# Softmax chains and filter taps in a streaming Conformer layer: negated scores, scaling on ScalarE, two banks in block one, a dearer tap behind the maxima

## Chip, cores and metric

One core of one Trainium2 chip. The metric is the device time of one execution in microseconds (us). Engines are TensorE (PE: matmuls; PEld: its weight loads), VectorE (DVE), ScalarE (ACT), GpSimd (POOL) and SyncE (SP, which issues the DMAs). Each engine works through its own instructions strictly in the order in which the program lists them; an instruction that has to wait holds up everything behind it on the same engine.

## What is computed

One layer of a streaming encoder, 2048 prompt tokens and 64 sample tokens, model width 1024, in fp32. The parts that matter here:

```python
u = glu_a * jax.nn.sigmoid(glu_b)                 # 512 channels
y = conv_general_dilated(concat(hist, u), w_dw)   # causal depthwise filter, 31 taps
y = jax.nn.silu(layer_norm(y + b_dw))             # norm over the 512 channels
conv_out = y @ w_out

s = einsum('bqhd,bkhd->bhqk', q, k) * ATTN_SCALE  # 8 heads of 64, ATTN_SCALE = 1/8
s = where(mask, s + rel_bias[...], NEG_INF)       # own chunk of 64 and the 8 chunks before
o = softmax(s) @ v
```

Both branches are gated, added and projected, and a SwiGLU network of inner width 2816 follows.

## The kernel before

**Tiling.** The 2112 tokens go in four blocks, 0 to 575 (sample and 512 prompt tokens) and then 512 each. In the first phase each block passes through the stages q, 0, k, 1, v, 2, 3, g: q, k, v are the attention projections, 0 to 3 are the four groups of 128 GLU channels, each followed by its filter (`convolve`), and g is the two sets of gates. Every fp32 product is three matmuls of high and low parts (`ps<-whi,hh`, `ps<-whi,hl`, `ps<-wlo,hh`), so PE is by far the most loaded engine. The second phase (merge, projections, SwiGLU) starts after the fourth block; the change touches none of its code.

**The filter.** Per block there are 120 taps behind the four first products, of 606 columns in block one (with the sample's and its history) and 512 elsewhere, one DVE instruction each (`y<-u,wd,y`), each reading the sum that the one before wrote. When all 120 of a block are done, `conv_norm` follows: POOL adds the four groups, PE takes the mean (`pm<-s,ones`), DVE subtracts it four times (`y<-y,pm`), ACT squares four times, POOL adds three times (`s<-s,ln`), and PE takes the second mean with a second `pm<-s,ones`.

**Attention.** A head has four query tiles of 128 (in the first block tile widths of 128, 256, 384 and 512 keys, elsewhere 640) and, in block one, a sample tile of 64. Per tile: PE writes the scores `sc`; DVE adds the bias to the score, scales by 0.125 and takes the row maximum, all in one instruction (`pr<-sc,bias`, result in `sm`), then multiplies the maximum by -1 (`sm<-sm`); ACT takes exp with its row sum (`pr<-pr,sm`); DVE inverts the sum and multiplies (`pr<-pr,sm`; in block four ACT does that); PE transposes (`ptp<-ident,pr`), ACT and DVE split that in high and low (`ph`, `pl`), and PE multiplies by the values (`po`). The score tile is one PSUM buffer of two banks, so the scores of a tile wait until the maximum of the tile before has read it. There are 32 such heads and 8 sample heads, 136 maxima in all.

**The order.** Nothing is scheduled at run time. While the program is written, `Stream` keeps a running load of each engine from a table of costs (a 512-wide tap counts 607 ns of DVE). Every 500 ns of PE load, `tick` lets five lanes issue what is due: token norms, projections' follow-up work, attention, the tail (`conv_norm`) and the filter. The filter lane issues up to four taps when the DVE load is less than 2000 ns ahead of PE; attention goes on when DVE is less than 3000 (2500 between score tiles) and ACT less than 4000 ahead. At stage 0 of a block everything left of the block before, taps and `conv_norm`, is forced out; at stage q the same happens with the token tiles not yet normalised (`x_t`). The tile scheduler below may still move instructions by priority.

Of the kernel before, what the change touches and what calls it, by code (L numbers as in the profile page):

```python
# [8 lines left out]
F32 = mybir.dt.float32  # L9
F32R = mybir.dt.float32r  # L10
AF = mybir.ActivationFunctionType
ALU = mybir.AluOpType
# [4 lines left out]
P = 128  # L17
# [26 lines left out]
PE_LAG = 400.0  # L44
TURN_LAG = 2500.0
KN_LAG = 5000.0
X_LAG = 8000.0
ON_ACT = (3,)
ON_POOL = ()
DMA_LAG = 4000.0  # L50
OUT_LAG = 4000.0
# [6 lines left out]
SCORE_ROOM = {"dve": 2500}  # L58
# [530 lines left out]
def streaming_layer(ctx: ExitStack, tc: tile.TileContext, I, O):  # L589
    nc = tc.nc  # L590
    stream = Stream()
    pe, dve, act, gps = (
        Meter(e, n, stream) for e, n in ((nc.tensor, "pe"), (nc.vector, "dve"), (nc.scalar, "act"), (nc.gpsimd, "pool"))
    )
# [44 lines left out]
    wd = const.tile([P, 4, TAPS], F32, name="wd")  # L639
# [90 lines left out]
    ps_a = p1.enter_context(tc.tile_pool(name="ps_a", bufs=1, space=PSUM))  # L730
    wk = p1.enter_context(tc.tile_pool(name="wk", bufs=1))
# [225 lines left out]
    bias = wk.tile([P, 640], F32, name="bias")  # L957
# [203 lines left out]
    def glu(b, ct):  # L1161
# [22 lines left out]
        W.done()  # L1184
        return u

    def convolve(u, y, ct, b):
# [12 lines left out]
        gps.tensor_copy(hist[:, ct], u[:, w - HIST : w])  # L1200
        dve.tensor_scalar(y[:, ct, :n], u[:, :n], wd[:, ct, 0:1], bdw[:, ct : ct + 1], ALU.mult, ALU.add)
        for k in range(1, TAPS):
            dve.scalar_tensor_tensor(y[:, ct, :n], u[:, k : k + n], wd[:, ct, k : k + 1], y[:, ct, :n], ALU.mult, ALU.add)
            yield

    def conv_norm(y, c0, n, t0):
# [91 lines left out]

    def softmax_max(ps, n, w, bias):
        pr = wk.tile([P, 640], F32, tag="pr", name="pr", bufs=8)  # L1300
        sm = wk.tile([P, 4], F32, tag="sm", name="sm", bufs=9)
        nb = ps.shape[1]
        stream.after("dve", "pe")
        dve.tensor_tensor_reduce(
            out=pr[:n, :w].rearrange("p (a b) -> p a b", a=nb), in0=ps, in1=bias.rearrange("p (a b) -> p a b", a=nb),
            scale=0.125, scalar=-3e38, op0=ALU.add, op1=ALU.max, accum_out=sm[:n, 0:1],
        )
        dve.tensor_scalar(sm[:n, 1:2], sm[:n, 0:1], -1.0, None, ALU.mult)
        free = stream.when("dve")
        stream.after("act", "dve")  # L1310
        act.activation(pr[:n, :w], pr[:n, :w], AF.Exp, bias=sm[:n, 1:2], accum_out=sm[:n, 2:3])
        return pr, sm, free, stream.when("act")

    def softmax_scale(pr, sm, n, w, on_act):
# [48 lines left out]
    def spans(b):  # L1363

        if b == "s":
            return 0, SMP, 0, CACHE + SMP
        past = QB if b else 0
        return SMP + QB * b, QB, CACHE + SMP + QB * b - past, QB + past
# [6 lines left out]
            )  # L1375
        return bias

    order, loaded, now = [], {}, {"scored": -1, "finished": -1, "bias": None}
# [21 lines left out]
    def attend(i):  # L1400
        x, h = order[i]
        q0, nq, k0, nk = spans(x)
# [5 lines left out]
        tiles = []  # L1408
        for t in range(0, nq, P):
            n = min(P, nq - t)  # L1410
            ps = ps_a.tile([P, 2, 512], F32, tag="s", name="sc")
            if x not in (0, "s"):
                for j in range(2):
                    for d in range(2):
                        pe.matmul(ps[:, j, :320], q2[:, d, t : t + P], kk[:, t + 320 * j : t + 320 * j + 320], start=d == 0, stop=d == 1)
                w, src, bs = 640, ps[:, :, :320], bias[:, ::-1]
            else:
                w = nk if x == "s" else t + P
                for d in range(2):
                    pe.matmul(ps[:n, 0, :w], q2[:, d, t : t + n], kk[:, :w], start=d == 0, stop=d == 1)  # L1420
                src, bs = ps[:n, 0:1, :w], bias[:n, 64:384][:, ::-1] if x == "s" else bias[:, :w][:, ::-1]
            pr, sm, free, ready = softmax_max(src, n, w, bs)
            tiles.append((pr, sm, n, w))
            if t + P < nq:
                yield free + PE_LAG, SCORE_ROOM
            else:
                fetch(i + 1)
                now["scored"] = i
            if t:
                softmax_scale(*tiles[-2], x in ON_ACT)  # L1430
        yield ready
        softmax_scale(*tiles[-1], x in ON_ACT)
        yield stream.when("act" if x in ON_ACT else "dve") + PE_LAG
        while now["finished"] < i - 1:
            yield lambda: now["finished"] == i - 1
        fetch_v(i + 1)
# [17 lines left out]
        else:  # L1454
# [15 lines left out]
            for jj in seq:  # L1470
# [11 lines left out]
                w = 512 - t0 * P  # L1482
# [39 lines left out]
    for b, stage in ORDER:  # L1522
# [60 lines left out]
    wk = ctx.enter_context(tc.tile_pool(name="wk2", bufs=1))  # L1583
# [136 lines left out]
    for s, (lo, hi) in enumerate(CBLOCKS):  # L1720
        tiles = token_tiles(lo, hi)
# [392 lines left out]
```

## Time and profile before

| | |
|---|---|
| median of 3 runs | 3046.8 us (3046.7 to 3047.27) |
| profiled execution | 3042.59 us, of which the span 3040.8 us |
| mean granted PE clock | 0.986 |
| PE busy | 2934.8 us (97% of the span) |
| PEld, DVE, ACT, POOL busy | 2606.5, 2052.4, 1256.8, 985.3 us |
| HBM traffic | 226 GB/s over the span |

The profile's windows give, for a stretch of time, how long each engine was busy and the clock granted to PE (1.00 is full, 0.50 half). Its waits name the tile that an idle engine waited for and the engine that released it. In the timeline a row has its start, its length, the engine and the instruction; square brackets hold the idle time ahead of it.

### The profile page before, as it was taken

The page shows a single profiled execution, that of the slowest core. Times are in us where ns is not written, and L with a number is a line of the kernel's source. Part 1 is how long each engine was busy: PE and PEld are TensorE (multiplying, and loading weights), DVE is VectorE, ACT ScalarE, POOL GpSimd, SP SyncE. Part 2 cuts the span into 40 slices and gives each one's busy share as a digit, 9 for nine tenths or more (in the row PEclk, how much of TensorE's full clock was granted, in tenths as well). Part 3 has the DMA queues.
Part 4 walks back from the last instruction along what each step waited for, and adds up shares of the span by engine and source line. Part 5 has one row for each costly group of instructions (what it writes and reads, how often), then busy time and mean ns, then how long its engine had stood idle before and what let it go on. Part 6 is the DMA issues. An engine that isn't in the chain of part 4 may idle for free. (4 is left out here: it accounts for less than half of the span.)

```text
span 3040.8 us, 44889 instructions
## 1 busy us (share of the span) xinstructions
PE 2934.8 (97%) x16259; PEld 2606.5 (86%) x16259; DVE 2052.4 (67%) x3835; ACT 1256.8 (41%) x2267; POOL 985.3 (32%) x617
## 2 busy tenths in 40 slices
PE   7989898999999999989999999999999999999998
PEld 4889776888888788878989889999999898999997
DVE  5896678777977895467666755655666756366567
ACT  3324532453254257464444425534444244333332
POOL 1200120101011102355677433247767341333331
PEclk9999998999999999999999999999999999999999
DMA  9888788888997788886444786455556965355554
GB/s 305 268 275 299 230 286 278 275 263 268 305 284 243 247 265 282 253 285 215 149 143 144 231 290 207 157 165 190 182 194 201 342 215 190 118 167 173 166 160 176
DMA packets 487019, 690.98 MB, mean 227 GB/s; under 512 B 38420, under 2 KB 316808, under 8 KB 486797
## 3 DMA queue, kind: packets, MB, share of 16 engines
q1 hardware_dynamic: 474517, 670.72, 67.3%
q10 hardware_dynamic: 12280, 17.39, 1.6%
q8 instruction: 128, 2.10, 0.3%
q14 instruction: 94, 0.77, 0.1%
HBM read 503.79 MB, written 184.19 MB: 226 GB/s over the span
## 5 line engine op out<-in xcount | busy, mean ns | idle before, releaser
L104 POOL TENSOR_TENSOR wlo<-wst,whi 128x1024 fp32r<-128x1024 f32 (+1 forms) x180 | 401.4, 2236 | 491.6 <-ACT whi L104 463.9
L104 PE MATMUL ps<-t,whi 128*128 128x384 f32 (+1 forms) x2112 | 506.1, 324 | 10.0 <-DVE t L104 4.8
L104 PE MATMUL pd<-whi,hid 128*128 128x512 f32 (+1 forms) x1400 | 450.2, 391 | 3.4 <-DVE acc L104 3.4
L104 ACT ACTIVATE whi<-wst 128x1024 fp32r<-128x1024 f32 (+1 forms) x273 | 266.1, 979 | 358.6 <-PE ps L104 123.7
L104 PE MATMUL ps<-b,whi 128*128 128x384 f32 (+1 forms) x1584 | 381.7, 326 | 11.0 <-DVE pw L104 4.0
L104 PEld LDWEIGHTS ps<-t,whi 128*128 128x128 f32 x2112 | 370.7, 189 | 18.4 <-DVE t L104 5.9
L104 DVE SCALAR_TENSOR_TENSOR y<-u,wd,y 128x512 f32<-128x512 f32 (+1 forms) x480 | 369.3, 772 | 6.7
L104 PE MATMUL ps<-hh,whi 128*128 128x512 f32 (+2 forms) x992 | 364.6, 367 | 0.7 <-DVE h L104 0.7
L104 PE MATMUL ps<-hl,whi 128*128 128x512 f32 (+2 forms) x992 | 348.1, 351 | 0.0
L104 PE MATMUL ps<-hh,wlo 128*128 128x512 f32 (+2 forms) x992 | 347.6, 350 | 0.0
L104 DVE TENSOR_TENSOR acc<-acc,pd 128x512 f32<-128x512 f32 (+1 forms) x440 | 290.7, 684 | 80.5 <-PE pd L104 76.9
L104 PE MATMUL ps<-t,wlo 128*128 128x384 f32 (+1 forms) x1056 | 340.8, 323 | 0.0
L104 PEld LDWEIGHTS pd<-whi,hid 128*128 128x128 f32 (+1 forms) x1400 | 258.1, 184 | 64.7 <-DVE acc L104 6.9
L104 PEld LDWEIGHTS ps<-b,whi 128*128 128x128 f32 x1584 | 278.7, 190 | 14.3 <-DVE pw L104 4.3
L104 PE MATMUL pd<-wlo,hid 128*128 128x512 f32 (+1 forms) x700 | 273.7, 391 | 0.0
L104 PE MATMUL ps<-b,wlo 128*128 128x384 f32 (+1 forms) x792 | 257.3, 325 | 0.0
L104 POOL TENSOR_TENSOR r<-t,mhalf 128x8 f32<-128x8 f32 (+3 forms) x68 | 84.4, 1243 | 390.0 <-DVE t L104 380.1
L104 PEld LDWEIGHTS ps<-hh,wlo 128*128 128x128 f32 x992 | 188.6, 190 | 22.7
L104 POOL TENSOR_TENSOR wlo<-wup,whi 128x1024 fp32r<-128x1024 f32 (+1 forms) x64 | 138.2, 2160 | 213.0 <-ACT whi L104 190.7
L104 PEld LDWEIGHTS ps<-hh,whi 128*128 128x128 f32 x992 | 189.3, 191 | 19.7 <-issue 1.9
L104 PEld LDWEIGHTS ps<-hl,whi 128*128 128x128 f32 x992 | 189.3, 191 | 15.5 <-issue 1.4
L104 PEld LDWEIGHTS ps<-t,wlo 128*128 128x128 f32 x1056 | 199.3, 189 | 0.6
(217 smaller groups left out, 5717.5 us busy)
## 6 DMA issues: line engine op xcount, KB each, us to landing
whi<-w_din_h SPq DMA_DIRECT2D x72, 512.0 KB, 5.8
wlo<-w_din_l SPq DMA_DIRECT2D x72, 512.0 KB, 7.0
wst<-sum_d SPq DMA_DIRECT2D x131, 256.0 KB, 2.9
wmod<-in_w_ada SPq DMA_DIRECT2D x48, 512.0 KB, 6.7
sum_d<-ws SPq DMA_DIRECT2D x88, 256.0 KB, 3.2
wst<-in_w_ffn_in SPq DMA_DIRECT2D x85, 256.0 KB, 3.4
wst<-in_w_in SPq DMA_DIRECT2D x40, 512.0 KB, 7.1
wst<-in_w_ffn_in SPq DMA_DIRECT2D x37, 512.0 KB, 5.3
```

The lines of the kernel that those rows point to most:

```text
L104: return f(*args, **kw)
```

## The change

1. The score instruction takes scale -0.125 and a minimum: the minimum of the negated scores is minus the maximum, so it is directly the bias of exp, which now runs with scale -1. 136 DVE instructions `sm<-sm` go.
2. The scaling by the inverted sum runs on ACT in all blocks: 104 `pr<-pr,sm` leave DVE and are added to ACT (64 of 128x640, the others in block one).
3. In block one a score buffer holds two tiles, one in each bank, and the second is emitted without waiting for the maximum of the first.
4. Each tap adds 110 ns to the emission's DVE load on top of its 607.
5. The first tap emitted after a maximum is told to stand behind that maximum on DVE; the taps after it follow, since they form a chain.

PE has the same 16027 instructions in another order, SP the same 1908. DVE goes from 3837 to 3599, ACT from 2176 to 2280, POOL from 622 to 620 (two `wlo` move to DVE).

```diff
-ON_ACT = (3,)
+    def behind(one):
+        return tc.issue_after(one.ins) if one is not None else nullcontext()
...
         for k in range(1, TAPS):
-            dve.scalar_tensor_tensor(y[:, ct, :n], u[:, k : k + n], wd[:, ct, k : k + 1], y[:, ct, :n], ALU.mult, ALU.add)
+            with behind(now.pop("least", None)):
+                dve.scalar_tensor_tensor(y[:, ct, :n], u[:, k : k + n], wd[:, ct, k : k + 1], y[:, ct, :n], ALU.mult, ALU.add)
+            stream.load["dve"] += 110.0
...
-        dve.tensor_tensor_reduce(
+        now["least"] = dve.tensor_tensor_reduce(
...
-            scale=0.125, scalar=-3e38, op0=ALU.add, op1=ALU.max, accum_out=sm[:n, 0:1],
+            scale=-0.125, scalar=3e38, op0=ALU.add, op1=ALU.min, accum_out=sm[:n, 0:1],
         )
-        dve.tensor_scalar(sm[:n, 1:2], sm[:n, 0:1], -1.0, None, ALU.mult)
...
-        act.activation(pr[:n, :w], pr[:n, :w], AF.Exp, bias=sm[:n, 1:2], accum_out=sm[:n, 2:3])
+        act.activation(pr[:n, :w], pr[:n, :w], AF.Exp, bias=sm[:n, 0:1], scale=-1.0, accum_out=sm[:n, 1:2])
...
-        dve.reciprocal(sm[:n, 3:4], sm[:n, 2:3])
-        if on_act:
-            stream.after("act", "dve")
-            act.activation(pr[:n, :w], pr[:n, :w], AF.Copy, scale=sm[:n, 3:4])
-        else:
-            dve.tensor_scalar(pr[:n, :w], pr[:n, :w], sm[:n, 3:4], None, ALU.mult)
+        stream.after("dve", "act")
+        dve.reciprocal(sm[:n, 2:3], sm[:n, 1:2])
+        stream.after("act", "dve")
+        act.activation(pr[:n, :w], pr[:n, :w], AF.Copy, scale=sm[:n, 2:3])
...
-            ps = ps_a.tile([P, 2, 512], F32, tag="s", name="sc")
+            if x != 0 or t % (2 * P) == 0:
+                both = ps_a.tile([P, 2, 512], F32, tag="s", name="sc")
+            ps = both if x != 0 or t % (2 * P) == 0 else both[:, 1:]
...
-            if t + P < nq:
+            if x == 0 and t % (2 * P) == 0:
+                yield stream.load["pe"], SCORE_ROOM
+            elif t + P < nq:
                 yield free + PE_LAG, SCORE_ROOM
```

How this moves instructions is seen at three places. The first is DVE at the first head of block two. `ISA pr,sm<-sc,bias` is the maximum (after the change, the minimum) of a score tile, `ISA sm` the reading of its accumulator, and `y<-u,wd,y` a tap. Before:

```order
L104 TENSOR_TENSOR A_173<-A_173,cols 128x2x2x2
L104 SCALAR_TENSOR_TENSOR y<-u,wd,y 128x512 x12
L104 ISA pr,sm<-sc,bias 128x640
L104 ISA sm 128x1
L104 SCALAR_TENSOR_TENSOR y<-u,wd,y 128x512
L104 TENSOR_SCALAR sm<-sm 128x1
L104 SCALAR_TENSOR_TENSOR y<-u,wd,y 128x512
L104 ISA pr,sm<-sc,bias 128x640
```

And now, at the same head:

```order
L103 SCALAR_TENSOR_TENSOR u<-tb,ps 128x512
L103 TENSOR_SCALAR y<-u,wd,cols 128x512
L103 COPY R<-pa 128x256
L103 TENSOR_TENSOR A_173<-pa,cols 128x2x2x2
L103 TENSOR_TENSOR A_173<-A_173,cols 128x2x2x2
L103 ISA pr,sm<-sc,bias 128x640
L103 ISA sm 128x1
L103 RECIPROCAL sm<-sm 128x1
L103 ISA pr,sm<-sc,bias 128x640
L103 ISA sm 128x1
L103 ISA pr,sm<-sc,bias 128x640
```

The run of twelve taps that stood directly ahead of the head's first maximum stands behind its maxima now.

The second place is PE at the end of stage q of block two, where the two means of block one's `conv_norm` stand (`pm<-s,ones`; `ps` are projections, `sc` scores of a head of block one). Before, the second mean stood here, 70 rows behind the first:

```order
L104 MATMUL ps<-whi,hh 128x512
L104 MATMUL ps<-wlo,hh 128x512
L104 MATMUL ps<-whi,hl 128x512
L104 MATMUL pm<-s,ones 128x512
L104 MATMUL sc<-kk,q_3947 128x256 x2
```

Now both stand here:

```order
L103 MATMUL ps<-whi,hl 128x512
L103 MATMUL pm<-s,ones 128x512
L103 MATMUL sc<-kk,q_4037 128x128 x2
L103 MATMUL sc<-kk,q_4037 128x256 x2
L103 MATMUL pm<-s,ones 128x512
L103 MATMUL ps<-hh,whi 128x512
```

Only two score tiles stand between the two means.

The third place is PE at the first head of block four. Before, six products stood between one score tile and the next:

```order
L104 MATMUL ps<-hh,wlo 128x512
L104 MATMUL sc<-kk,q_10960 128x320 x4
L104 MATMUL ps<-hh,whi 128x512
L104 MATMUL ps<-hl,whi 128x512
L104 MATMUL ps<-hh,wlo 128x512
L104 MATMUL ps<-hh,whi 128x512
L104 MATMUL ps<-hl,whi 128x512
L104 MATMUL ps<-hh,wlo 128x512
L104 MATMUL sc<-kk,q_10960 128x320 x4
```

Now all four score tiles (16 matmuls) stand together, with the first transposes behind them:

```order
L103 MATMUL ps<-hh,wlo 128x512
L103 MATMUL sc<-kk,q_10838 128x320 x16
L103 MATMUL ptp<-ident,pr 128x128 x2
L103 MATMUL pt<-ident,u 30x128
L103 MATMUL ptp<-ident,pr 128x128 x6
L103 MATMUL ps<-hh,whi 128x512
```

The products that lay between the score tiles stand ahead of them and behind the transposes.

More of the change, by code (lines that the diff above doesn't have):

```diff
@@ L1185, in glu @@
         return u
+    now = {"scored": -1, "finished": -1, "bias": None}
+    def behind(one):
+        return tc.issue_after(one.ins) if one is not None else nullcontext()
     def convolve(u, y, ct, b):
@@ L1300, in softmax_max, with softmax_scale @@
         pr = wk.tile([P, 640], F32, tag="pr", name="pr", bufs=8)
-        sm = wk.tile([P, 4], F32, tag="sm", name="sm", bufs=9)
+        sm = wk.tile([P, 3], F32, tag="sm", name="sm", bufs=9)
         nb = ps.shape[1]
         stream.after("dve", "pe")
-        dve.tensor_tensor_reduce(
+        now["least"] = dve.tensor_tensor_reduce(
             out=pr[:n, :w].rearrange("p (a b) -> p a b", a=nb), in0=ps, in1=bias.rearrange("p (a b) -> p a b", a=nb),
-            scale=0.125, scalar=-3e38, op0=ALU.add, op1=ALU.max, accum_out=sm[:n, 0:1],
+            scale=-0.125, scalar=3e38, op0=ALU.add, op1=ALU.min, accum_out=sm[:n, 0:1],
         )
-        dve.tensor_scalar(sm[:n, 1:2], sm[:n, 0:1], -1.0, None, ALU.mult)
         free = stream.when("dve")
         stream.after("act", "dve")
-        act.activation(pr[:n, :w], pr[:n, :w], AF.Exp, bias=sm[:n, 1:2], accum_out=sm[:n, 2:3])
+        act.activation(pr[:n, :w], pr[:n, :w], AF.Exp, bias=sm[:n, 0:1], scale=-1.0, accum_out=sm[:n, 1:2])
         return pr, sm, free, stream.when("act")
-    def softmax_scale(pr, sm, n, w, on_act):
-        dve.reciprocal(sm[:n, 3:4], sm[:n, 2:3])
-        if on_act:
-            stream.after("act", "dve")
-            act.activation(pr[:n, :w], pr[:n, :w], AF.Copy, scale=sm[:n, 3:4])
-        else:
-            dve.tensor_scalar(pr[:n, :w], pr[:n, :w], sm[:n, 3:4], None, ALU.mult)
+    def softmax_scale(pr, sm, n, w):
+        stream.after("dve", "act")
+        dve.reciprocal(sm[:n, 2:3], sm[:n, 1:2])
+        stream.after("act", "dve")
+        act.activation(pr[:n, :w], pr[:n, :w], AF.Copy, scale=sm[:n, 2:3])
     def load_qk(h, q0, nq, k0, nk):
@@ L1376, in load_bias @@
         return bias
-    order, loaded, now = [], {}, {"scored": -1, "finished": -1, "bias": None}
+    order, loaded = [], {}
     def attention(b):
@@ L1429, in attend @@
             if t:
-                softmax_scale(*tiles[-2], x in ON_ACT)
+                softmax_scale(*tiles[-2])
         yield ready
-        softmax_scale(*tiles[-1], x in ON_ACT)
-        yield stream.when("act" if x in ON_ACT else "dve") + PE_LAG
+        softmax_scale(*tiles[-1])
+        yield stream.when("act") + PE_LAG
         while now["finished"] < i - 1:
```

## The prediction

> **What bounds the kernel now.** I read the page first, then the windows, then the waits of PE, and then the timeline at each long wait.
>
> ```profile
> span 3040.8 us, 44889 instructions
> PE 2934.8 (97%) x16259; PEld 2606.5 (86%) x16259; DVE 2052.4 (67%) x3835; ACT 1256.8 (41%) x2267; POOL 985.3 (32%) x617
> PE 40%; DVE 1%; DMA 1%; issue 0%; ACT 0%; POOL 0%; SPq 0%; DVEq 0%; POOLq 0%; ACTq 0%
> ```
>
> PE is busy for 2934.8 of 3040.8 us and holds nearly all of the chain that ended last. The change leaves PE its 16027 instructions. So the time can only change where PE stands idle (106 us in all) or runs at half clock; DVE and ACT work counts only where PE waits for it.
>
> ```profile
> 190.00:300.00 110.00, 102.71 (x717) 97.51 (x718) 85.23 (x194) 45.39 (x106) 3.32 (x8) 0.94 0.85 284
> 300.00:400.00 100.00, 88.88 (x525) 74.80 (x524) 70.55 (x184) 51.95 (x116) 22.70 (x23) 0.93 0.79 261
> 400.00:500.00 100.00, 92.40 (x466) 72.86 (x466) 75.22 (x166) 27.24 (x65) 10.23 (x9) 0.93 0.92 291
> 500.00:600.00 100.00, 91.01 (x479) 75.19 (x478) 82.95 (x169) 36.26 (x66) 8.07 (x8) 0.95 0.77 253
> 600.00:700.00 100.00, 98.95 (x577) 85.59 (x576) 71.46 (x177) 52.42 (x109) 14.42 (x12) 1.00 0.87 272
> 800.00:900.00 100.00, 99.19 (x527) 82.05 (x526) 85.57 (x165) 41.72 (x75) 13.96 (x12) 1.00 0.90 273
> ```
>
> The columns are window, length, busy PE, PEld, DVE, ACT, POOL, clock, DMA share and GB/s. From 190 to 600 PE misses 7.29 + 11.12 + 7.60 + 8.99 = 35 us and the clock is 0.93 to 0.95. From 600 on it misses one per cent at full clock. The attention of the first blocks is where something can be had; the attention of blocks three and four can only lose.
>
> ```profile
> PE sc L104 <- DVE sm L104: 19.8, 8, 8.0
> PE ptp L104 <- DVE pr L104: 5.0, 4, 3.3
> PE ps L104 <- ACT hh L104: 4.8, 1, 4.8
> PE pt L104 <- DVE x_t L104: 3.5, 1, 3.5
> ```
>
> These are PE's waits from 190 to 620 (total, times, longest). 24.8 us are softmax chains, the rest of the list is the token norm of the next block. I call the five places A (187.8), E (352.4), B (422.7), C (477.3) and D (505), and ask for each stretch:
>
> ```profile
> 187.82:201.00 13.18, 4.99 (x15) 3.08 (x15) 12.74 (x32) 3.74 (x10) 0.00 (x0) 0.62 1.02 376
> 352.40:363.00 10.60, 2.26 (x10) 1.85 (x10) 5.45 (x15) 5.01 (x13) 3.94 (x4) 0.61 1.07 300
> 422.70:430.00 7.30, 3.43 (x11) 2.43 (x11) 5.57 (x17) 2.58 (x7) 0.70 (x1) 0.76 0.27 78
> 477.30:485.00 7.70, 4.37 (x16) 3.12 (x15) 6.24 (x15) 1.63 (x5) 1.13 (x2) 0.75 1.01 405
> 505.00:516.00 11.00, 2.09 (x6) 1.69 (x7) 10.61 (x21) 0.96 (x3) 0.00 (x0) 0.66 0.29 105
> ```
>
> A stretch costs its idle time, and what its matmuls lose to the half clock: nothing of the busy time at least, half of it at most. A: 8.2 to 10.7, E: 8.3 to 9.5, B: 3.9 to 5.6, C: 3.3 to 5.5, D: 8.9 to 10.0. Together 32.6 to 41.3 us, middle 37.
>
> At D the cause is plain, and at A it is of the same kind:
>
> ```profile
> 187.89 5.26 DVE L104 SCALAR_TENSOR_TENSOR y<-u,wd,y 128x606 f32<-128x606 f32 x6
> 193.06 0.28 DVE L104 CUSTOM_DVE_ANT_0 pr<-sc,bias 128x128 f32<-128x128 f32 x1
> 193.41 0.79 PE L104 MATMUL sc<-kk,q 128*128 128x256 f32 x2 [5.59 <-DVE sm L104]
> ```
> ```profile
> 502.77 9.41 DVE L104 SCALAR_TENSOR_TENSOR y<-u,wd,y 128x512 f32<-128x512 f32 x12
> 512.10 0.82 DVE L104 CUSTOM_DVE_ANT_0 pr<-sc,bias 128x640 f32<-128x640 f32 x1
> 512.98 1.43 PE L104 MATMUL sc<-kk,q 128*128 128x320 f32 x4 [8.00 <-DVE sm L104]
> ```
>
> Six taps (5.26 us), and twelve (9.41 us), stood on DVE ahead of the maximum for which the second score tile waits. At C the taps stand between the steps of a sample tile's chain:
>
> ```profile
> 477.51 0.48 DVE L104 CUSTOM_DVE_ANT_0 pr<-sc,bias 64x320 f32<-64x320 f32 x1
> 480.17 0.37 DVE L104 TENSOR_SCALAR pr<-pr,sm 64x320 f32<-64x320 f32 x1
> 480.69 0.36 PE L104 MATMUL ptp<-ident,pr 64*128 64x64 f32 x3 [3.33 <-DVE pr L104]
> ```
>
> **The change, part by part.** The prices:
>
> ```profile
> L104 DVE SCALAR_TENSOR_TENSOR y<-u,wd,y 128x512 f32<-128x512 f32 x360 | 268.4, 748 | 4.8
> L104 DVE CUSTOM_DVE_ANT_0 pr<-sc,bias 128x640 f32<-128x640 f32 x96 | 78.6, 819 | 26.2 <-PE sc L104 23.2 <-DMA bias<-rb_d 1.1 <-PE ptp L104 1.0
> L104 DVE TENSOR_SCALAR pr<-pr,sm 128x640 f32<-128x640 f32 x64 | 38.1, 595 | 0.8
> L104 DVE TENSOR_SCALAR sm<-sm 128x1 f32<-128x1 f32 x128 | 18.9, 148 | 1.0
> L104 ACT ACTIVATE pr<-pr,sm 128x640 f32<-128x640 f32 x128 | 104.6, 827 | 104.2 <-DVE sm L104 102.9 <-ACT gate L104 0.8
> L104 ACT ACTIVATION_READ_ACCUMULATOR pr<-pr,sm 128x1 f32 x128 | 23.9, 187 | 0.0
> L104 DVE TENSOR_SCALAR h<-pt,A,B 128x128 f32<-128x128 f32 x107 | 37.4, 401 | 4.1 <-PE pt L104 4.1
> L104 DVE TENSOR_TENSOR y<-y,pm 128x512 f32<-128x512 f32 x16 | 9.9, 681 | 1.3 <-PE pm L104 1.3
> L104 ACT ACTIVATE hh<-h 128x512 fp32r<-128x512 f32 x24 | 14.8, 626 | 12.2 <-DVE h L104 10.6 <-PE ps L104 1.5
> L104 POOL TENSOR_TENSOR s<-s,ln 128x512 f32<-128x512 f32 x12 | 15.6, 1297 | 83.7 <-ACT ln L104 83.4
> L104 POOL TENSOR_TENSOR r<-t,mhalf 128x8 f32<-128x8 f32 x32 | 61.0, 1906 | 146.9 <-DVE t L104 145.5 <-DVE sm L104 1.4
> ```
>
> PE's pace, for work in its order, is that of two products in a row, 0.23 us from start to start:
>
> ```profile
> 502.20 0.39 PE L104 MATMUL ps<-hh,whi 128*128 128x512 f32 x1
> 502.43 0.39 PE L104 MATMUL ps<-hl,whi 128*128 128x512 f32 x1
> ```
>
> *Negated scores and scaling on ACT.* DVE loses 18.9 us of `sm<-sm`, 38.1 of `pr<-pr,sm` at 128x640, and the smaller shapes; ACT gains 64 x 0.83 = 53 us at 128x640. ACT is busy for 41% of the span, DVE for 67%, PE's work lies over both, so by themselves these are worth nothing outside the waits. Inside a chain the negation saves 0.15 us per tile, while the scaling costs 0.827 on ACT where it cost 0.595 on DVE: 0.23 more, but no longer behind taps. Taken as zero per tile; bounds -0.15 and +0.23 over 104 tiles if every chain were exposed, so -16 and +24, and hardly any is. Freeing DVE should shorten the small waits between the five places. Idle time there is 35 - 32.6, some 3 us on the lower counting, and I take 2 of it.
>
> *Taps behind maxima, and the 110.* They take the taps away from B, C and D. At B the first two scores of the head now stand earlier, 24 us of PE work ahead of the next two: saved 4.7 (middle). At C eleven taps instead of nineteen stand between two maxima, and some 20 matmuls of 0.23 us stand between scores and transposes where one stood: saved 4.4. At D no tap stands ahead of or between the four maxima. Late next are the maxima themselves: each further score tile waits for 0.82 + 0.08 us, and a reciprocal that waits for exp (0.83 + 0.19) stands ahead of the second. So 3 us stay: 9.4 - 3 = 6.4 saved. At A, with its two banks, a filter's first product and two `wlo` stand ahead of the first minimum instead of six taps, but now all four scores and ten transposes stand together with nothing in between, so that the whole chain of four tiles is exposed. I leave 7.4 of 9.4: saved 2, bounds 0 and 5.
>
> *What is forced out later.* A dearer tap means that fewer are emitted per step: the taps of block one end ten maxima later, and its `conv_norm` falls to the end of stage q of block two, where it is forced. The two `pm` stand two score tiles apart (six short matmuls). Between them must run on DVE the first two of the four `y<-y,pm` (2 x 0.68), ACT's square of the second (0.6, as `hh` of the same size), then three `s<-s,ln` on POOL (3 x 1.30), with an `r<-t,mhalf` of 1.91 between the second and third: 1.4 + 0.6 + 3.9 + 1.9 = 7.8 us, less 0.4 of PE work, plus 1 by half clock: **8.4 lost**. Least would be 5 (if `r` is done early), most 11.
>
> E is replaced: the third tile of tokens (`x_t`) still has its DMA six SP issues behind a head's q and k loads, instead of ten, and its eight transposes stand directly before products that need them; I leave 7 of 8.9, saved 2. The fourth tile's eight transposes now stand directly before its products in blocks two, three and four, where there were products between them: eight `h` at 0.40 us on DVE, the first four of which and a split (0.6) PE must await: 2.2 us, three times: **6.6 lost**, bounds 2 and 10.
>
> *First heads and the last.* At block four's first head the four score tiles stand together, where six products lay between them. Three waits of 0.9 us, and 2 us at the transposes: 4.7 lost. The last head's 20 transposes stand 1.4 us of work behind its scores, where 6.1 us stood: 3 lost. Both are bounded by 2 and 10 together with the clock.
>
> The sum: saved 4.7 + 4.4 + 6.4 + 2 + 2 + 2 = 21.5; lost 8.4 + 6.6 + 4.7 + 3 = 22.7. The profiled execution of 3042.6 would become **3043.8**, and with the 4.2 us by which the median lies above the profiled one, 3048.
>
> [...] At B a longest wait of 3.21 us goes with a clock of 0.76 over 7.3 us (the stretches above). [...]
>
> **The rivals.**
>
> *F, faster: the late work overlaps.* The waits of stage q follow each other within some 20 us. While PE stands at `pm`, DVE and ACT finish the fourth tile's norm, so that its 2.2 goes; and with A's chain at its better bound (3 more), E gone (7 more) and first heads free of waits (4), the sum is 16 better: some 3032. For it: DVE is 57 us less busy. Against it: an engine in strict order waits itself, for PE's `pm`.
>
> *S, slower: ACT becomes the bound of exposed heads.* Four tiles of exp, accumulator and scaling take 4 x (0.83 + 0.19 + 0.83) = 7.4 us of ACT behind the first maximum, where the DVE scaling ran beside exp. Where only some 4 us of PE work stands between the last score and the last transposes (first heads of blocks two, three and four, the head before stage q's end, the last) this adds 3 us each, with the clock 4: five times, 15 to 20, so some 3065. It decides from the point at which those heads have less PE work than ACT needs. For it: all scores at A, D and the first head of block four are contiguous. Against it: ACT stands idle for 104.2 us ahead of these instructions.
>
> *N: the order doesn't help.* If B, C and D wait for something else that the releaser hides (the projection's `u`, a bias DMA), 15.5 saved are gone: 3063.
>
> **How the numbers follow.** My forecast (3048, own range 3038 to 3058) has 0.42, F 0.30, S 0.20, N 0.08. The range takes F's better part and S's: 3018 to 3076. A measurement of this kernel can tell about 0.2% (6 us) from no change. Faster by more than that: F, and a quarter of the forecast's chance: 0.40. Within: half of the forecast's chance and a little of F: 0.23. Slower: the rest, 0.37.
>
> **What the new profile would show.** D: the wait of 8.00 gone, two or three of 0.9 to 1.5 in its place. C and B: no wait over 1 us. Near the end of stage q of block two: a wait of `pm` for POOL's `s` of 6 to 9 us, the longest of the run. Block four's first head: three waits `sc<-sm` of 0.9. If ACT `pr` is named ahead of many `ptp`, S holds. The prediction is wrong if `pm` isn't waited for, or if PE loses more than 10 us from 600 to 1225 beside what it lost.

## The result

| kernel | median, us | ratio to before, 95% interval |
|---|---|---|
| before | 3046.8 (15 runs) | |
| changed | 3053.7 (15 runs) | 1.0024 (1.0017 to 1.0031) |

The change costs 7 us. The profiled execution of the changed kernel took 3055.7 us, 13.1 more than that of before; half of that difference is not the change's doing, as the table of losses below shows. Its page:

```profile
span 3053.9 us, 44730 instructions
PE 2942.5 (96%) x16259; PEld 2613.0 (86%) x16259; DVE 2001.3 (66%) x3597; ACT 1323.4 (43%) x2371; POOL 975.0 (32%) x615
PE 40%; DVE 1%; DMA 1%; issue 0%; ACT 0%; POOL 0%; SPq 0%; DVEq 0%; POOLq 0%
```

DVE is busy for 51 us less and ACT for 67 more, as the instruction counts had it, and PE still holds the chain. The windows answer those of before:

```profile
190.00:300.00 110.00, 104.32 (x739) 98.92 (x740) 86.24 (x170) 57.07 (x130) 2.53 (x5) 0.97 0.85 280
300.00:400.00 100.00, 82.81 (x449) 70.57 (x449) 66.24 (x162) 53.74 (x123) 22.59 (x27) 0.88 0.75 247
400.00:500.00 100.00, 97.26 (x534) 76.35 (x533) 78.93 (x154) 34.88 (x75) 11.33 (x11) 1.00 0.90 295
500.00:600.00 100.00, 97.27 (x513) 79.33 (x513) 75.24 (x141) 49.72 (x87) 7.22 (x8) 1.00 0.93 294
```

From 400 to 600 PE gained 11 us of busy time, at full clock; from 300 to 400 it lost 6 and clock. The end of the first phase, half of block four, is where the rest went. The first line below is of before, the second of the changed kernel:

```profile
1040.00:1226.00 186.00, 183.99 (x961) 154.92 (x959) 140.04 (x290) 109.91 (x190) 22.38 (x16) 1.00 0.85 270
```
```profile
1040.00:1237.00 197.00, 184.34 (x932) 153.77 (x930) 134.66 (x251) 108.51 (x188) 22.73 (x16) 0.97 0.80 249
```

The same stretch of the program takes 197 us with 12.7 of idle time, where it took 186 with 2.0.

For all kernels of this study I add up the idle time of PE and half of the time for which it was busy at half clock, between the same products of the main loop, from each trace. "Start" ends at some 185 us, ahead of the first head; "four" is split at 1040 us of before. The last column is the total; the spans less this total agree within 2 us of 2911 for before, changed and the fastest kernel of the study, so this is where the difference lies. The half is an estimate: in the trace of before two products of 512 columns in a row start 0.43 us apart at half clock (363.32 and 363.75) and 0.23 at full clock (502.20 and 502.43).

| lost by PE, us | start | block one | stage q of block two | rest of two | three | four, to 1040 | four, rest | second phase | total |
|---|---|---|---|---|---|---|---|---|---|
| before | 22.3 | 15.2 | 13.6 | 26.5 | 1.8 | 5.5 | 2.3 | 41.8 | 129 |
| changed | 28.8 | 12.8 | 21.1 | 6.1 | 6.7 | 4.2 | 18.6 | 43.8 | 142 |

Each row is one execution, and the start tells how far one execution can be trusted. Its losses all lie in PE's first 564 matmuls, which are the same in every kernel of this study, and yet these losses go from 19.9 to 29.4 us over the 14 traces: 19.7 to 22.1 of idle time, and 0 to 7.9 by half clock. So the 6.5 us between the two starts above are no part of the change.

The waits of PE over the whole of the changed kernel (those of its start and of the second phase left out):

```profile
PE sc L103 <- DVE sm L103: 10.9, 12, 3.8
PE sc L103 <- DMA kk<-k_d: 8.9, 6, 2.2
PE ps L103 <- ACT hh L103: 8.3, 5, 2.4
PE pt L103 <- DVE x_t L103: 8.1, 6, 2.2
...
PE pm L103 <- POOL s L103: 5.9, 3, 3.2
...
PE ptp L103 <- ACT pr L103: 4.5, 8, 1.0
```

The scores' waits for a maximum fell from 19.8 to 10.9 us and the longest from 8.0 to 3.8. The waits for the loads of the keys (`kk`) grew from 2.3 to 8.9 us, and the norm's mean (`pm`) is new on the list. The transposes' wait for the scaled tile, 5.6 us behind DVE's `pr` before, is 4.5 behind ACT's.

### The profile page after: what moved, and what is told of

Same layout as the page of the kernel before. It is cut to its first block, busy times and chain, and to the rows that moved or that the text cites. A ratio compares the mean times of both kernels' runs of the same rounds, so it can differ in the third digit from the quotient of the medians.

```text
span 3053.9 us, 44730 instructions
## 1 busy us (share of the span) xinstructions
PE 2942.5 (96%) x16259; PEld 2613.0 (86%) x16259; DVE 2001.3 (66%) x3597; ACT 1323.4 (43%) x2371; POOL 975.0 (32%) x615
## 5 line engine op out<-in xcount | busy, mean ns | idle before, releaser
L103 PE MATMUL ps<-b,whi 128*128 128x384 f32 (+1 forms) x1584 | 382.1, 327 | 10.9 <-DVE pw L103 4.0
L103 ACT ACTIVATE pr<-pr,sm 128x640 f32<-128x640 f32 (+3 forms) x272 | 200.8, 747 | 145.7 <-DVE sm L103 142.9
L103 PEld LDWEIGHTS ps<-hh,whi 128*128 128x128 f32 x992 | 189.9, 191 | 19.7 <-issue 2.4
```

What stands on the lines that cost most here:

```text
L103: return f(*args, **kw)
```

## The experiments

Every kernel was timed beside the kernel before on the same chip, with medians of before from 3045.7 to 3046.8. The medians of two kernels are compared in the text; the ratios, which weigh all runs of a kernel against those of before on the same chip, put some of these differences lower, and where that matters it is said. Theory E says that the emission decides: taps behind the maxima gain, a dearer tap packs other work together and loses. Theory S says that ScalarE's scaling is the loss. A table of all losses by stage stands behind the twelfth run.

**The extra cost not in block four.**

```diff
-            stream.load["dve"] += 110.0
+            stream.load["dve"] += 110.0 if b < 3 else 0.0
```

> The changed kernel, with the extra 110 ns of a tap left out in block four alone; its order up to block four's first filter is that of the changed kernel. In the profile of the changed kernel PE loses 12.7 us idle and some 6 us by half clock from 1040 us to the end of the first phase, where the kernel before lost 2.3 and 0. Theory E (the dearer tap packs block four's heads together: four score tiles in a row, q and k loads late): most of these 16 us come back, so 10 to 16 us below the changed kernel, some 3040, 4 to 8 below the kernel before. Theory S (the scaling and its place on ScalarE make exposed heads longer): block four scaled on ScalarE before already, so nothing of it differs; 0 to 3 us come back.

3039.3 us, ratio 0.9977 (0.9968 to 0.9986): 14.4 below the changed kernel, as theory E had it. Windows of the same stretch, and the only wait of PE that is listed for it:

```profile
1034.00:1219.00 185.00, 182.35 (x959) 154.67 (x957) 140.16 (x259) 110.55 (x191) 22.62 (x16) 1.00 0.86 271
```
```profile
PE sc L103 <- DVE sm L103: 0.3, 1, 0.3
```

Idle time falls from 12.7 to 2.7 us, the clock is whole again, and the loads of the keys no longer come late. Ahead of that stretch, block four loses 5 us more than in the changed kernel (9.2 for 4.2). Up to block four's first filter the two kernels are the same program, and their losses from block one to block three differ by up to 2.6 us: less than that in a single stage says nothing.

**The extra cost nowhere.**

```diff
-            stream.load["dve"] += 110.0
```

> The changed kernel without the extra 110 ns in any block: taps are emitted as early as before, still behind the maxima. Theory E: block four as in the run above (10 to 16 us back), and the two means of block one's norm stand 19 us of work apart again, so the wait of pm for s near 386 us (3.2) and that of sc ahead of it (3.8) with their half clock (some 4) go: another 5 to 10, but the filters' taps come back ahead of some maxima (6 ahead of one at block three, 4 at block four's first head): 2 to 5 lost. In sum 12 to 20 below the changed kernel: some 3037, 10 below the kernel before. Theory S: within 4 us of the changed kernel.

3035.4 us, 0.9959 (0.9946 to 0.9973): 18.3 below the changed kernel, inside theory E's range. Stage q of block two loses 6.6 us instead of 21.1. The rest of block two loses 15.4 instead of 6.1, and block one itself 18.9 instead of 12.8: there the dearer tap is worth something.

**The rule left out.**

```diff
-            with behind(now.pop("least", None)):
+            if True:
```

> The changed kernel without the rule that a tap stands behind the maximum emitted ahead of it; the 110 stays. In the order 12 taps stand directly ahead of block two's first maximum again, 7 ahead of the very first and 7 ahead of block four's first. Theory E: D comes back at its length before (8.0 us of wait and 2 of half clock, less the 2.0 that stay now): 7 to 8 lost, A 2 to 4 lost, block four's first head 3 to 5 more: 12 to 17 us above the changed kernel, some 3067. Rival: the taps' place doesn't matter, since DVE has 57 us less to do and gets through them in time: within 3 us of the changed kernel.

3063.0 us, 1.0055 (1.0043 to 1.0068): 9.3 above the changed kernel. At block two's first head:

```profile
503.03 9.41 DVE L103 SCALAR_TENSOR_TENSOR y<-u,wd,y 128x512 f32<-128x512 f32 x12
...
512.36 0.82 DVE L103 CUSTOM_DVE_ANT_0 pr<-sc,bias 128x640 f32<-128x640 f32 x1
...
513.24 1.44 PE L103 MATMUL sc<-kk,q 128*128 128x320 f32 x4 [8.00 <-DVE sm L103]
```

D is back to the hundredth (8.00 us), though DVE has its 51 us less to do. So a shorter queue does not help a maximum that stands behind twelve taps. I expected block four to lose 3 to 5 as well; it lost 11.3 instead of 18.6, which is why the sum stayed below 12.

**The scaling back on VectorE in blocks one to three.**

```diff
-        stream.after("act", "dve")
-        act.activation(pr[:n, :w], pr[:n, :w], AF.Copy, scale=sm[:n, 2:3])
+        if on_act:
+            stream.after("act", "dve")
+            act.activation(pr[:n, :w], pr[:n, :w], AF.Copy, scale=sm[:n, 2:3])
+        else:
+            dve.tensor_scalar(pr[:n, :w], pr[:n, :w], sm[:n, 2:3], None, ALU.mult)
...
-        softmax_scale(*tiles[-1])
-        yield stream.when("act") + PE_LAG
+        softmax_scale(*tiles[-1], x == 3)
+        yield stream.when("act" if x == 3 else "dve") + PE_LAG
```

> The changed kernel with the scaling of blocks one to three back on VectorE (595 ns for 128x640 there, against 827 on ScalarE). The taps' cost, the negated scores, the two banks and the rule stay. Theory E: the places move (the two means of block one's norm stay 1.9 us of work apart), the sum hardly: within 5 us of the changed kernel, block four's first head 3 to 6 better as its four score tiles don't stand in one row. Theory S: the chains shorten by 0.23 us a tile and ScalarE's queue by 57 us: 8 to 15 us below the changed kernel.

3036.5 us, 0.9964 (0.9952 to 0.9976): 17.2 below the changed kernel, beyond either. But 12.8 of it stand in the rest of block four (5.8 lost instead of 18.6), whose own scaling didn't change: its heads are no longer packed, presumably since the emission reaches them with other loads. This run can't tell the two theories apart; the eighth can.

**The rule alone, in the kernel before.**

```diff
+            with behind(now.pop("least", None)):
...
-        dve.tensor_tensor_reduce(
+        now["least"] = dve.tensor_tensor_reduce(
```

> The kernel before with one part of the change alone: the first tap emitted after a maximum stands behind that maximum. No taps stand directly ahead of the very first maximum (6 before) nor of block two's first (12 before); the two means of block one's norm stay 15.4 us of work apart, block four's first head stays spread. Theory E (the rule is what gains, the dearer tap what loses): A, C and D give back 10 to 17 us: 3030 to 3037. Rival (the gain needs a VectorE that has less to do): 0 to 4 us below the kernel before, since its 57 us more of work now stand elsewhere in the same chains.

3036.3 us, 0.9972 (0.9961 to 0.9983): 9.4 below before on the same chip (3045.7), at the lower edge of what theory E had. The rest of block two falls from 26.5 to 13.8. One part of the change is a gain by itself.

**One tile per score buffer.**

```diff
-            if x != 0 or t % (2 * P) == 0:
-                both = ps_a.tile([P, 2, 512], F32, tag="s", name="sc")
-            ps = both if x != 0 or t % (2 * P) == 0 else both[:, 1:]
+            if True:
+                both = ps_a.tile([P, 2, 512], F32, tag="s", name="sc")
+            ps = both
...
-            if x == 0 and t % (2 * P) == 0:
-                yield stream.load["pe"], SCORE_ROOM
-            elif t + P < nq:
+            if t + P < nq:
```

> The changed kernel with one query tile per score buffer in block one, as before. The means of block one's norm stand 6.5 us of work apart instead of 1.2. Theory E: A's four scores wait for each other's maxima, 2 to 4 us lost there; the wait of sc (3.8) and pm (3.2) near 386 us shrinks by 3 to 6; block four stays as it is in the changed kernel. In sum within 4 us of the changed kernel, 3050 to 3057. Rival (two banks are worth a chain's length at each of block one's eight heads): 6 to 12 us above it.

3046.0 us, 0.9995 (0.9986 to 1.0004): 7.7 below the changed kernel, neither of the two. In the changed kernel the two banks lose: with one, block one loses 15.1 us instead of 12.8, but stage q of block two 17.3 instead of 21.1 and the rest of two 2.6 instead of 6.1.

**The extra cost in blocks two and three alone.**

```diff
-            stream.load["dve"] += 110.0
+            stream.load["dve"] += 110.0 if b in (1, 2) else 0.0
```

> The changed kernel with the extra 110 ns of a tap in blocks two and three alone. Theory E: the means of block one's norm stand 19.2 us of work apart again, so PE loses at stage q of block two what it lost in the run without any extra (6.6 us) and not what it lost in the one without it in block four (20.5), but some 4 more ahead of it, as there: 8 to 11 below that one, some 3030, and 5 or so below the run without any extra, since the three filters behind keep their order. Rival (where the taps of block one go is of no account, its stalls come back elsewhere): as the run without it in block four, 3037 to 3041.

3031.7 us, 0.9960 (0.9947 to 0.9972): 7.6 below the run without it in block four, a little under theory E's 8 to 11, and level with the run without any (3.7 by the medians, nothing by the ratios, 0.9960 and 0.9959). Stage q of block two loses 5.5 us and block one 20.4, as in the run without any (6.6 and 18.9), where the run without it in block four has 20.5 and 10.5. So in block one the dearer tap gains some 9 us, and pays some 15 for them at stage q.

**The same with the scaling of blocks one to three on VectorE.** The edits of the fourth and the seventh run together.

> The run before in this list, with the scaling of blocks one to three on VectorE. Theory E: the place of the scaling is worth little by itself: within 4 us of the run with the scaling on ScalarE. Theory S: 8 to 15 us below it, near 3018, as four tiles of exp and scaling would be 7.4 us of ScalarE behind the first maximum of each head.

3017.8 us, 0.9916 (0.9901 to 0.9930): 13.9 below the seventh run and 28 below before, the fastest kernel of the study. Theory S is right in size here, theory E wrong. But the mechanism is not the one I gave it: in the seventh run PE waits for ScalarE's scaling (`ptp` behind ACT's `pr`) for 1.8 us in all, from 190 to 1220.

```profile
PE ps L103 <- ACT hh L103: 7.4, 4, 2.4
PE pm L103 <- POOL s L103: 6.2, 2, 5.5
PE sc L103 <- DMA kk<-k_d: 6.0, 7, 2.1
...
PE ptp L103 <- ACT pr L103: 1.8, 5, 0.6
```

What it waits for is other work. In the eighth run (190 to 1200) the key loads are gone from the list, and the waits for the mean fall to 2.7, while those for a maximum grow from 3.2 to 8.3 and those for `x_t` from 1.5 to 4.0:

```profile
PE sc L103 <- DVE sm L103: 8.3, 9, 2.8
PE ps L103 <- ACT hh L103: 5.0, 6, 2.2
PE pt L103 <- DVE x_t L103: 4.0, 1, 4.0
PE pm L103 <- POOL s L103: 2.7, 2, 2.3
```

One of these waits can be followed, the split `hh` of block three's tokens. In the seventh run:

```profile
665.77 2.31 DVE L103 TENSOR_SCALAR h<-pt,A,B 128x128 f32<-128x128 f32 x7
665.89 1.55 ACT L103 ACTIVATE pr<-pr,sm 128x640 f32<-128x640 f32 x2
667.34 0.61 ACT L103 ACTIVATE hh<-h 128x512 fp32r<-128x512 f32 x1
...
668.00 0.50 PE L103 MATMUL ps<-whi,hh 128*128 128x512 f32 x1 [1.98 <-ACT hh L103]
```

Two scalings stand on ScalarE ahead of `hh`, but they hardly delay it: of the seven `h` on DVE, some 0.32 us apart, `hh` reads the first four, the last of which ends at 667.12, 0.2 us before `hh` starts. In the eighth run `hh` (658.15) has projection work (`kn`) and no scaling directly ahead of it, and PE waits half as long:

```profile
657.68 0.59 ACT L103 ACTIVATE kn<-ps 128x512 f32<-128x512 f32 x1
...
658.15 0.63 ACT L103 ACTIVATE hh<-h 128x512 fp32r<-128x512 f32 x1
...
658.84 0.49 PE L103 MATMUL ps<-whi,hh 128*128 128x512 f32 x1 [0.97 <-ACT hh L103]
```

So what differs is the order of the work around the wait, and why VectorE is the better place for the scaling stays open. That it is holds in three pairs of runs: 17.2 us between the changed kernel and the fourth run, 13.9 here, and 6.0 without any extra cost (the second run and the tenth below).

**The rule and the negated scores, in the kernel before.** The rule's edit as in the fifth run, and:

```diff
-            scale=0.125, scalar=-3e38, op0=ALU.add, op1=ALU.max, accum_out=sm[:n, 0:1],
+            scale=-0.125, scalar=3e38, op0=ALU.add, op1=ALU.min, accum_out=sm[:n, 0:1],
...
-        dve.tensor_scalar(sm[:n, 1:2], sm[:n, 0:1], -1.0, None, ALU.mult)
...
-        act.activation(pr[:n, :w], pr[:n, :w], AF.Exp, bias=sm[:n, 1:2], accum_out=sm[:n, 2:3])
+        act.activation(pr[:n, :w], pr[:n, :w], AF.Exp, bias=sm[:n, 0:1], scale=-1.0, accum_out=sm[:n, 2:3])
```

> The kernel before with two parts: taps behind the maxima, and negated scores (136 short VectorE instructions less). The scaling is as before, one tile per score buffer, no extra cost of a tap. The order stands close to that of the rule alone (3036.3). Theory E (an instruction taken off VectorE is worth only what its chain's exposure is): 0 to 4 us below the rule alone, 3032 to 3037. Rival (each of 136 negations at 0.15 us lies on PE's path): 15 to 20 us below it.

3047.7 us, 0.9999 (0.9991 to 1.0008): 11.4 above the rule alone (8 by the ratios), where both expectations had it below. Taking 136 instructions off VectorE cost time. The rest of block two loses 23.2 instead of 13.8: 3.1 us more of idle time and 6.3 more by half clock. The longest wait there is in a sample tile's chain:

```profile
472.19 0.74 DVE L104 SCALAR_TENSOR_TENSOR y<-u,wd,y 128x512 f32<-128x512 f32 x1
...
473.06 0.73 DVE L104 SCALAR_TENSOR_TENSOR y<-u,wd,y 128x512 f32<-128x512 f32 x1
473.71 0.37 DVE L104 TENSOR_SCALAR pr<-pr,sm 64x320 f32<-64x320 f32 x1
...
474.23 0.55 PE L104 MATMUL ptp<-ident,pr 64*128 64x64 f32 x3 [3.44 <-DVE pr L104]
```

This is C of the kernel before, with taps between the steps again and a wait of 3.44. The rule only moves taps behind a maximum, not behind the steps that follow it. But the rule alone has such a wait as well, of 3.23 us at 443.90, so this chain doesn't make the difference; the losses come from several smaller waits and the clock behind them, and which change of the order causes them was not found.

**The fastest without any extra cost.**

```diff
-            stream.load["dve"] += 110.0 if b in (1, 2) else 0.0
```

> The fastest kernel so far (3017.8: scaling on VectorE in blocks one to three, two banks, negated scores, the rule, the extra 110 ns in blocks two and three) without the 110 in any block. If the 110 is worth something there because it keeps taps from between the heads of blocks two and three: 3 to 8 us above it, 3021 to 3026. If it was only ever a loss: 0 to 5 below it.

3029.4 us, 0.9944 (0.9928 to 0.9959): 11.6 above it (8.5 by the ratios). The dearer tap gains in blocks two and three, more than expected: block three loses 8.4 us without it and 1.6 with it, block four's first half 6.6 against 1.9.

**The fastest with one bank.** The edit of the sixth run.

> The fastest kernel so far with one query tile per score buffer in block one. The two means of block one's norm stand 15.5 us of work apart, as before the change, so nothing is packed there. If two banks gain where no stall hides it: A's chain and block one's other heads lose 3 to 8 us, 3021 to 3026. If they gain nothing, as in the run with one bank in the changed kernel (7 us below the changed kernel): 3012 to 3018.

3034.7 us, 0.9959 (0.9947 to 0.9971): 16.9 above it (13 by the ratios), more than twice what was expected. The same two banks that lost 7.7 us in the changed kernel gain 16.9 here. But block one itself loses less with one bank (9.6 for 12.5): the difference stands at stage q of block two (19.0 for 11.0) and in block three (10.3 for 1.6), whose heads have one tile per buffer in both kernels. So what the two banks gain here, too, comes by the order.

**The fastest with block one's scaling on ScalarE.**

```diff
-softmax_scale(*tiles[-2], x == 3)
+softmax_scale(*tiles[-2], x in (0, "s", 3))
...
-yield stream.when("act" if x == 3 else "dve") + PE_LAG
+yield stream.when("act" if x in (0, "s", 3) else "dve") + PE_LAG
```

> The fastest kernel so far with the scaling of block one (and, as ever, block four) on ScalarE, that of blocks two and three on VectorE. It tells where the 14 us between ScalarE and VectorE come from. By the stages of the two profiles, idle plus half clock, blocks two and three (from 640 to 1030 us) account for 10 of them, block one and stage q behind it for 3. Theory Q (in blocks two and three a block's next token tiles wait on ScalarE's queue behind the scalings): 3 to 5 above the fastest, 3021 to 3023. Rival (the tight heads of block one set it): 10 to 14 above, 3028 to 3032.

3027.8 us, 0.9935 (0.9923 to 0.9946): 10.0 above it, the lower edge of the rival; by the ratios it is 5.8, and no expectation had that. Block one itself loses 19.5 instead of 12.5. It does so in the other two pairs with no extra cost in block one (20.4 for 12.5 in the seventh and eighth run, 18.9 for 13.1 in the second and tenth), and each time stage q of block two gives 3 to 6 of it back. So ScalarE's scaling does cost block one 6 to 8 us, but how the 14 us between the two places divide is not settled: 10 and 4 by the medians, 6 and 8 by the ratios.

| lost by PE, us | start | block one | stage q of block two | rest of two | three | four, to 1040 | four, rest | median |
|---|---|---|---|---|---|---|---|---|
| 1, no extra in four | 25.4 | 10.5 | 20.5 | 8.7 | 6.1 | 9.2 | 3.1 | 3039.3 |
| 2, no extra | 24.1 | 18.9 | 6.6 | 15.4 | 5.0 | 5.1 | 3.3 | 3035.4 |
| 3, no rule | 28.7 | 14.0 | 23.2 | 17.3 | 7.3 | 4.1 | 11.3 | 3063.0 |
| 4, scaling on DVE | 26.1 | 13.8 | 19.5 | 8.0 | 3.0 | 2.7 | 5.8 | 3036.5 |
| 5, rule alone | 26.1 | 11.2 | 13.7 | 13.8 | 2.6 | 4.6 | 3.5 | 3036.3 |
| 6, one bank | 24.1 | 15.1 | 17.3 | 2.6 | 7.0 | 5.9 | 17.6 | 3046.0 |
| 7, extra in two, three | 21.2 | 20.4 | 5.5 | 9.8 | 6.4 | 7.5 | 3.1 | 3031.7 |
| 8, and scaling on DVE | 19.9 | 12.5 | 11.0 | 9.7 | 1.6 | 1.9 | 3.5 | 3017.8 |
| 9, rule and negation | 29.4 | 11.2 | 14.6 | 23.2 | 4.2 | 5.9 | 2.3 | 3047.7 |
| 10, 8 without extra | 29.1 | 13.1 | 11.0 | 10.8 | 8.4 | 6.6 | 3.7 | 3029.4 |
| 11, 8 with one bank | 23.1 | 9.6 | 19.0 | 8.9 | 10.3 | 3.1 | 3.2 | 3034.7 |
| 12, 8, ACT in one | 29.0 | 19.5 | 7.7 | 8.2 | 2.8 | 3.5 | 3.5 | 3027.8 |

The dearer tap, the two banks and the scaling on ScalarE were not run each alone in the kernel before.

## Why the prediction was right, step by step

The forecast was 3048 with gains and losses of some 22 us each; the time is 3053.7. It lies in the forecast's own range (3038 to 3058), but the forecast was of a change of 1 us and the measured one is 7. One of the signs that it named for being wrong did come: from block three to the end of the first phase PE loses 20 us more than before (29.5 for 9.6), where it allowed 10. The other, that `pm` isn't waited for, did not come, though the wait for `pm` is 3.16 us and not 6 to 9. Where the terms went:

- **B, C, D: right.** I had 4.7 + 4.4 + 6.4, and 2 for small waits. The rest of block two went from 26.5 to 6.1, 20.4 saved. From 400 to 500, where B and C stood, no wait is over 0.9 us. At D two waits stay, as foreseen, of 1.01 and 1.03 us:

```profile
502.51 0.82 DVE L103 CUSTOM_DVE_ANT_0 pr<-sc,bias 128x640 f32<-128x640 f32 x1 [3.28 <-PE sc L103]
...
503.40 0.86 PE L103 MATMUL sc<-kk,q 128*128 128x320 f32 x4 [1.01 <-DVE sm L103]
...
505.29 0.86 PE L103 MATMUL sc<-kk,q 128*128 128x320 f32 x4 [1.03 <-DVE sm L103]
```

At D the rule does this, as the third run showed. Of the whole 20.4 it makes some 11 to 13: left out, 17.3 are lost instead of 6.1 (third run), and alone it brings 26.5 to 13.8 (fifth run). The dearer tap makes the rest: without it 15.4 are lost (second run).

- **The norm's two means, E and the fourth tile in stage q of block two: right.** I had 8.4 + 2.2 - 2 = 8.6 lost; it is 7.5 (13.6 to 21.1). The chain stands in the trace as the order had it, and the wait is shared between a score and the second mean:

```profile
381.53 2.47 DVE L103 TENSOR_TENSOR y<-y,pm 128x512 f32<-128x512 f32 x4
383.55 2.62 POOL L103 TENSOR_TENSOR s<-s,ln 128x512 f32<-128x512 f32 x2 [5.28 <-ACT ln L103]
385.10 0.79 PE L103 MATMUL sc<-kk,q 128*128 128x256 f32 x2 [3.81 <-DVE sm L103]
386.12 1.64 POOL L103 TENSOR_TENSOR r<-t,mhalf 128x8 f32<-128x8 f32 x1
387.73 1.26 POOL L103 TENSOR_TENSOR s<-s,ln 128x512 f32<-128x512 f32 x1
389.05 2.08 PE L103 MATMUL pm<-s,ones 128*128 128x512 f32 x2 [3.16 <-POOL s L103]
```

3.81 + 3.16 = 6.97 us of wait. The `r` between the last two sums is the one that was counted. The second and seventh run take the cause, the 110 in block one, away, and stage q falls to 6.6 and 5.5. That the same 110 gains 6 to 8 us in block one (12.8 lost, against 18.9 and 20.4) the prediction didn't see.

- **Fourth tiles of blocks three and four: right.** 2.2 each predicted, 2.03 and 1.99 measured (`ps` behind `hh`). Behind the first of them stands half clock, 1.7 us, for which the sum had nothing; more on this in the last section.

- **A: the number right by luck.** I had 2 saved of 9.4, 5 at best. PE's idle time at the very first head is 3.6 us (187.8 to 200) where it was 8.2, and with the half clock behind it A went from 12.5 to 6.1, so 6.4 are saved. But in the rest of block one the losses rose from 2.7 to 6.8; most of this is a wait of 2.0 us for the sample's mean (`pm` behind POOL's `s`, at 312.9) and 1.7 of half clock behind it, which the prediction didn't have. Together 15.2 became 12.8, 2.4 saved.

- **First heads and the last: the foreseen waits right, the size not.** I had 4.7 + 3 us; it is 16.3 (2.3 to 18.6), 10.4 of idle time and 5.9 by half clock. The three waits at block four's first head are 0.92 each, but a load of the keys stands ahead of them, and the half clock behind:

```profile
1064.70 0.85 PE L103 MATMUL sc<-kk,q 128*128 128x320 f32 x4 [1.91 <-DMA kk<-k_d]
...
1066.47 1.13 PE L103 MATMUL sc<-kk,q 128*128 128x320 f32 x4 [0.92 <-DVE sm L103]
...
1068.52 1.44 PE L103 MATMUL sc<-kk,q 128*128 128x320 f32 x4 [0.92 <-DVE sm L103]
...
1070.88 1.44 PE L103 MATMUL sc<-kk,q 128*128 128x320 f32 x4 [0.92 <-DVE sm L103]
```

PE waits for such loads three times in this stretch, 6.0 us in all. The step followed DVE and PE there and left SP's queue out, though the packing that it read off the order also moves each head's loads. What delayed them was not tried by itself; the first run shows that with block four's taps at their old cost they are in time. At the first head SP issued the second of its two key loads at 1053.78, 10.9 us ahead of the scores and 12 behind the first, with stores of `v` between them; before, the two went out together, some 15 us ahead. The lead is not all of it: at the head near 1146 it is 9.3 us, with a wait of 2.2, where before it was 6.2, with none.

- **The scaling: wrong as a term, though it doesn't show in the sum.** "Worth nothing outside the waits" holds for the chains themselves, but the eighth run puts 13.9 us on its place, spread over a late mean, late key loads and late splits. Rival S had the size, but not the mechanism: its sign, ACT's `pr` ahead of many `ptp`, makes 1.8 us in the seventh run, and 4.5 in the changed kernel where DVE's `pr` made 5.6 before. In the changed kernel itself the price is masked: the fourth run's gain stands mostly in block four.

- **The negation: wrong.** Together with the scaling it was bounded at -16 to +24 us, with the gain on its side, and taken as zero. It cost 11.4 beside the rule (ninth run). A chain that got shorter by an instruction can't explain that; that the places which the emission then chose do is argued, not shown.

The profiled execution lies 2 us above the median and 11.9 above the 3043.8 of the sum. The first and last heads are 8.6 of it. The start, where PE's first 564 matmuls are the same as before, is 6.5 (22.3 to 28.8), of which 5.7 is half clock: the spread of single executions. The other terms make up -3.2. So the errors of the terms come to 5.4 us, about what the medians show (3053.7 for 3048).

## What to carry to other kernels

When a program's order is written by a planner with its own costs, no edit is only its instructions: here the same two banks cost 7.7 us in one setting and gain 16.9 in another, and 136 instructions less on an engine off the critical path cost 11. Compare the two orders first, look at each place where waiting work has become contiguous, and price it from the trace's chain, with the queue that brings its data. Compare stages of two traces only beyond what the same code varies by from one execution to the next: here 9.5 us at the start and 2.6 in a later stage. Then test the parts one by one and in pairs: one part alone gave 9 of the 28 us that the best combination gave, while the whole change lost 7.

## What the runs showed of the hardware

The clock after a gap is not a matter of the gap's length alone. In the changed kernel the same wait for `hh` stands at the start of blocks three and four, 2.03 and 1.99 us long:

```profile
674.00:682.00 8.00, 5.97 (x22) 4.57 (x21) 6.18 (x19) 3.82 (x7) 1.64 (x1) 0.79 0.65 168
956.00:964.00 8.00, 6.01 (x28) 4.88 (x28) 5.90 (x16) 3.87 (x7) 1.64 (x1) 1.00 0.73 217
```

The first left a clock of 0.79 over 8 us, the second one of 1.00. The traces' records of the granted clock tell why. In one execution the clock changed only at the edges of steps of 3.41 us: in the trace of the changed kernel the half clock came 17 times, 8 times for 3.41 us, 5 times for 6.83, 3 times for 10.24, and once to the end of the trace. All edges of a trace fit one grid within 3 ns, and the grid lay elsewhere in each execution (its first edge 3.25 us behind the span's start in the trace of before, 1.90 in that of the changed kernel). The first gap (674.47 to 676.51) lay within one step, 674.33 to 677.74, and at 677.74 the clock fell to half for one step. The second (956.14 to 958.12) lay across the edge at 957.63: 1.49 us of idle time in the one step, 0.49 in the next.

I counted idle time by such steps in all 14 traces, from 25 us on and where the clock was whole. Behind each of the 132 steps with 2.0 us or more of idle time the clock fell, behind none of the 11736 with less than 1.1, and behind 61 of the 174 between. In the traces of before and of the changed kernel alone it fell behind all 20 steps with 2.0 us or more and behind 7 of the 21 between; the least idle time behind which it fell there was 1.65 us, in three gaps (the changed kernel, 189.64 to 193.05), and the most behind which it didn't was 1.93, in one gap (before, 112.48 to 115.89). So in these traces the clock fell behind 1.1 to 2.0 us of idle time in one step, about half of it, in one gap or several. Whether a gap of 2 us cost 1.7 us more (an estimate: half of a busy step of 3.41) depended on where the grid lay in that execution.
